# Moving one tile's loads to another queue, cutting the decays in two, and putting additions behind others, in a two-layer trunk of attention and RWKV-7

## The chip, the cores and the metric

The kernel runs on one core of a Trainium2 chip. The metric is the device time of one execution in microseconds (us), and of a few runs the median counts. Engines are named as in the profile: PE is TensorE, DVE is VectorE, ACT is ScalarE, POOL is GpSimd, SP is SyncE.

## The reference

One sequence of 512 tokens with 2048 channels, float32, goes through two residual layers, each `x + W_out(mixer(rms_norm(x)) * silu(gate))`.

```
# layer 0: differential attention, 8 heads of two 128-wide queries and keys, values 256 wide
proj = h @ w_in ; q, k, v, gate = split(proj, 4)
q, k = rope(rms_norm(q)), rope(rms_norm(k))
a = softmax(q0 k0 + causal) - lam * softmax(q1 k1 + causal)
o = rms_norm(a @ v) * (1 - lambda_init) * silu(gate) ; out = o @ w_out
# layer 1: RWKV-7, 32 heads of 64 channels
p = h @ w_in ; p = p + (token_shift(p) - p) * mu ; r, k, v, g, dw, da = split(p)
decay = exp(-exp(-softplus(-(w0 + tanh(dw) @ decay_up)) - 0.5)) ; a = sigmoid(a0 + da @ iclr_up)
kk = normalised(k * k_k) ; k = k * (1 + (a - 1) * k_a)
for each token:  S = S * w_t + (S a_t) b_t + v_t k_t ;  y_t = S r_t     # a_t = -kk, b_t = kk * a
y = group_norm(y) + sum(r * k * r_k) * v ; out = (y * silu(g)) @ w_out
```

## The kernel before

**Matmuls in three parts.** Every operand is split into a high part in the matmul's own format and a low remainder, and a product is three matmuls (high by high, low by high, high by low). For a weight chunk of 512 KB (`wraw`), ACT casts the high part (`wh`, L105) and DVE subtracts to get the low one (`wl`, L106). SP loads the chunks (`load_w`, L78), and POOL's queue makes additions in flight: `add_w` (L86) issues a DMA that adds a second weight chunk onto one that lies in SBUF.

**Layer 0** goes head by head. In `unit_head` the queries, keys, values and gates of one head are formed with seven products of half-size blocks in place of eight, so sums of weight blocks are wanted. The tiles Ta to Td (`g.Ts`) hold a chain of such sums: a product is made with T, then another block is added onto T, and the next product uses it. `all_groups` runs one product over the four chunks i of the contraction, and issues behind chunk i the additions for what comes next: onto T (`then`), and, in the last head alone, onto the four chunks of `b22` too (`also`). POOL issues them in the order in which they are written, since each is put behind the one before (`issue_after`).

While a head's products run on PE, the attention of the head before is woven in by a `Chain`: a generator that counts PE's matmuls and runs its next step when the count is through. `attention` works on four blocks of 128 rows; each step for a block has scores, transposes (L364), the weighted values, and `turn_y`, which writes the turned output as `yTh` (ACT, L399) and `yTl` (DVE, L401) and stores both on ACT's queue (L386) to the HBM tensors `ys`. `yTh` and `yTl` have one buffer each. A further chain (`keys`) turns the new keys with transposes at L296; its delay in matmuls is an argument, 9 and in the last head 20.

**Layer 1** goes over 16 pairs of heads. Pair j's projections fill PE; among them stand the scan of pair j − 1 (`scan_pair`, woven in by a chain: per chunk of 64 tokens the matmuls L1475, L1486 and L1493, and the state's update on DVE, L1497, which the next L1475 needs) and the preparation of pair j + 1.

- `stage1` makes the decays. The list `g.later` holds parts that are run one by one between the chain's steps, each behind the state's update on DVE (0) or ACT's copy (1): `decays` (the scan L1240 and the centring L1242, L1243), `exponentials` (ACT), `queries` (DVE, L1252 to L1254), `scales` (ACT, L1258), `keys` (L1262, L1266 and others).
- `gram` makes the Gram matrix `G` and stores blocks of it to HBM (`ltd`, L1316); `mask_gram` masks it in two halves on POOL (L1325, L1327).
- `t_solve` loads `ltd` back as the tile `LT`, rearranged, with four DMAs on POOL's queue (L1350), and solves a triangular system on DVE in 31 steps of two instructions (L1361, L1363), which end with L1364. The result goes to HBM (`td`, L1365), and `t_combine` loads it as `TT` and transposes it (L1388) for the matmuls L1394 and L1404. The second half of `mask_gram` stands behind the LT loads on POOL.
- `stage_v` makes y (L1418), `finish_y` ends a pair (L1547, L1554).

The Tile framework orders each engine's instructions by the priorities that the code gives (`high_priority` with offsets; the solve has the highest) and by `issue_after`, which puts one instruction behind another.

Of the kernel before, what the change touches and what calls it, by code (L numbers as in the profile page):

```python
# [28 lines left out]
NH = 8  # L29
# [44 lines left out]
def load_w(g, raw, part, k0, ks, queue=None):  # L74

    w, c = part
    with g.tc.issue_after(g.last) if g.last and not queue else ExitStack():
        ld = (queue or g.nc.sync).dma_start(out=raw[:, ks.start : ks.stop], in_=w[c][:, k0 + ks.start : k0 + ks.stop])  # L78
    g.last = ld.ins if g.last and not queue else g.last
    return ld.ins  # L80


def add_w(g, raw, part, k0):

    w, c = part
    return g.nc.gpsimd.dma_start(out=raw[:], in_=w[c][:, k0 : k0 + KG], accum_op=ALU.add).ins  # L86
# [378 lines left out]
KG = 2  # L465
# [66 lines left out]
def unit_head(g, aps, h, t1s, sq, turned):  # L532


    nc = g.nc
# [37 lines left out]
    def all_groups(out, lhs, raw, start=False, end=False, then=None, also=None):  # L573
        added = None
        for i in range(N):
            r = raw(i)
            products(out, lhs(i), r, start and i == 0, end and i == N - 1)
            for x, k0 in [(r, then)] + ([(also[i], (c2, 0))] if also else []) if then else []:
                with g.tc.issue_after(added) if added else ExitStack():
                    added = add_w(g, x, k0[0], k0[1] + i * KG)  # L580

    def s4(out, keep, start=False, end=False):
        def raw(i):
# [212 lines left out]
def layer0(g, aps):  # L796
# [3 lines left out]
    with ExitStack() as cx:  # L800
# [91 lines left out]
        for h in range(NH):  # L892
            if h:
                Chain(g, attention(g, h - 1, *before, 26, keys=rest), 56 if h > 1 else 20)
            t1s = [t1_tile() for _ in range(NT)] if h else t1s
            sq = g.small.tile([P, NT, 2], F32, name="sq", tag="sq")
            qkT = head_qkT(g)

            def keys(n, t1s=t1s, qkT=qkT):
                for t in range(n):  # L900
                    turn_qk(g, t1s, *qkT, t)
                    if t < n - 1:
                        yield 20

            rest = [(g, t1s, *qkT, t) for t in (2, 3)]
            if h:
                values = unit_head(g, aps, h, t1s, sq, lambda: Chain(g, keys(2), 9 if h < NH - 1 else 20))
            else:
                for ts in ([0, 1], [2, 3]):
                    head_qk(g, t1s, sq, ts)  # L910
                Chain(g, keys(2), 120)
                input_sums(g, pairs, False)
                ps = unit_tok(g, g.hH, g.hL, vg_cols(aps, h), 512)
                acc1 = g.work.tile([P, 2, 512], F32, name="acc1", tag="acc1", bufs=1)
                G, vg = gates(g)
# [298 lines left out]
def stage1(g, j, k, up):  # L1214
# [3 lines left out]
    p = Pair()  # L1218
# [20 lines left out]
    def decays():  # L1239
        nc.vector.tensor_tensor_scan(l[:].rearrange("p c t -> p (c t)"), g.rmask[:].rearrange("p c t -> p (c t)"),  # L1240
                                     lw[:], 0.0, ALU.mult, ALU.add)
        nc.vector.tensor_scalar(m[:], l[:, :, C - 1], 0.5, None, ALU.mult)  # L1242
        nc.vector.tensor_sub(l[:], l[:], m[:, :, None].to_broadcast([P, NC_, C]))  # L1243

# [21 lines left out]
        nc.vector.tensor_add(p.gam[:, 0 : NC_ - 1], m[:, 0 : NC_ - 1], m[:, 1:NC_])  # L1266
        nc.scalar.activation(p.gam[:, 0 : NC_ - 1], p.gam[:, 0 : NC_ - 1], AF.Exp)

    g.later += [(0, decays), (1, exponentials), (0, queries), (1, scales), (1, keys)]
    return p  # L1270


# [68 lines left out]
def t_solve(g, j, p):  # L1341
# [5 lines left out]
    Tm = w.tile([P, NQ, HALF], F32, name="Tm", tag="Tm", bufs=1)  # L1347
    tmp = w.tile([P, NQ * HALF], F32, name="tmpl", tag="tmpl", bufs=1)
    for i in range(NG):
        ld = nc.gpsimd.dma_start(out=LT[i * 32 : i * 32 + 32], in_=g.ltd[j % 2].rearrange("b h c s t -> (b h c) s t"))  # L1350
    n2 = LT[:, HALF, :]
    nc.vector.tensor_scalar(n2, n2, 1e-24, None, ALU.max)
    nc.vector.reciprocal(n2, n2)
# [9 lines left out]
        nc.vector.tensor_add(Tm[:, 0:s, i + 1 :], Tm[:, 0:s, i + 1 :], tt)  # L1363
    nc.vector.tensor_mul(Tm[:], Tm[:], n2[:, None, :].to_broadcast([P, NQ, HALF]))  # L1364
    nc.sync.dma_start(out=g.td[j % 2].rearrange("q l t -> l q t"), in_=Tm[:])  # L1365
    return ld.ins


GAP_D, GAP_X, GAP_T = 18, 10, 8
# [189 lines left out]
def layer1(g, aps):  # L1559
    nc, tc = g.nc, g.tc  # L1560
    with ExitStack() as cx:
# [25 lines left out]
        for j in range(D // P):  # L1587
# [15 lines left out]
            def behind(m, j=j, p=p, normed=normed):  # L1603
                if j > 1:
                    pairs[j - 2].chain.finish(g)
                with tc.issue_after(m.ins):
                    gram(g, j, p, j > LAG + 1 and pairs[j - 1].chain)
                p.rfs = split_act(g, p.rf[:], w, "x")
                mask_gram(g, p, 0)
                loaded = t_solve(g, j, p)  # L1610
                with tc.issue_after(loaded):
                    mask_gram(g, p, 1)
                if j > 1 and not normed:
                    group_norm(g, j - 2, pairs[j - 2])

# [6 lines left out]
                first = gate_of(0, "g0")  # L1622
            if j + 1 < D // P:
                begin(j + 1)
            if j > LAG:
                gated(g, j - LAG, pairs[j - LAG], gate_of(j - LAG))
            if j + 1 < D // P:
# [80 lines left out]
def body(ctx, tc, nc, aps):  # L1708
    g = Ctx()
    g.nc, g.tc = nc, tc  # L1710
    g.last, g.first, g.centred = None, [], None
    g.chains, g.later, g.state, g.copied = [], [], None, None
    g.const = ctx.enter_context(tc.tile_pool(name="const", bufs=1))
    g.hp = ctx.enter_context(tc.tile_pool(name="hp", bufs=16))
# [57 lines left out]
```

## Time and profile before

| | |
|---|---|
| median of 3 runs | 2111.32 us (2108.85 to 2113.85) |
| the profiled execution, its own time | 2111.84 us |
| its span | 2110.1 us |
| PE busy | 2076.8 us, 98% |
| DVE, ACT, POOL busy | 1602.6, 1153.6, 370.4 us |
| moved by DMA | 294.60 MB, 140 GB/s over the span |

The profile is of one execution. Span is the time from its first instruction to its last, and its own time stands beside it. A busy engine executes instructions; waiting, branching and issuing DMAs aren't counted. Where a row has a bracket, the engine was idle for so long ahead of it, and the name in it is what came last of that for which it waited.

### The profile page before, as it was taken

To read this page: it belongs to the slowest core of one execution; us is meant where nothing else is said; L and a number is where in the kernel's file an instruction comes from. 1 tells how busy PE (TensorE), PEld (TensorE's weight loads), DVE (VectorE), ACT (ScalarE), POOL (GpSimd) and SP (SyncE) were. 2 spreads that over 40 slices of the span, in tenths; PEclk is the share of its full clock that TensorE was granted. 3 is DMA by queue.
4 is the path that set the end of the run, shared out by engine and by line. 5 is a ranking of instruction groups with operands and counts; after the bars stand their busy time and mean duration, and the time that the engine had idled before them with its cause. 6 is when DMAs were issued, how large, how long until landed. Compare 5 with 4: busy or idle time off the path is not lost.

```text
span 2110.1 us, 34038 instructions
## 1 busy us (share of the span) xinstructions
PE 2076.8 (98%) x11852; PEld 1690.5 (80%) x11852; DVE 1602.6 (76%) x4129; ACT 1153.6 (55%) x2278; POOL 370.4 (18%) x727
## 2 busy tenths in 40 slices
PE   9999999999999999999999999999999999999999
PEld 7888888888887788878777778888877787877887
DVE  6988888889887876576777778877777887767645
ACT  5765656566565544355465555565555556555322
POOL 1021111201112000101122221222222122221001
PEclk9999999999999999999999999999999999999999
DMA  8487877878778946623232332323333232345655
GB/s 268 153 173 190 181 170 187 166 188 177 173 183 176 307 149 179 150 88 96 90 87 89 90 90 84 94 83 92 99 95 86 85 94 86 97 138 180 190 159 121
DMA packets 159484, 294.60 MB, mean 140 GB/s; under 512 B 64352, under 2 KB 81760, under 8 KB 159312
## 3 DMA queue, kind: packets, MB, share of 16 engines
q1 hardware_dynamic: 110848, 184.91, 28.1%
q0 software_dynamic: 23808, 83.54, 21.5%
q10 hardware_dynamic: 24656, 23.97, 3.5%
q8 instruction: 93, 1.52, 0.3%
q14 instruction: 79, 0.65, 0.1%
HBM read 268.71 MB, written 23.66 MB: 139 GB/s over the span
## 4 chain that ended last, share of the span: by engine, by line
PE 74%; DVE 17%; issue 3%; ACT 3%; DMA 2%; ACTq 0%; DVEq 0%; SPq 0%
PE pp L122 33%; PE pp L568 22%; PE pt L122 4%; DVE wl L106 4%; DVE tmpl L1361 3%; DVE Tm L1363 2%; DVE VS L1497 2%; PE gp L1304 1%; ACT wh L105 1%; PE sc L122 1%; PE o L122 1%; PE sm L1475 1%; PE lora L122 1%; PE z L122 1%; PE sm L1486 1%
## 5 line engine op out<-in xcount | busy, mean ns | idle before, releaser
L106 DVE TENSOR_TENSOR wl<-wraw,wh 128x1024 fp32r<-128x1024 f32 (+2 forms) x291 | 357.7, 1229 | 211.0 <-ACT wh L105 202.2
L105 ACT CAST wh<-wraw 128x1024 fp32r<-128x1024 f32 (+2 forms) x291 | 303.6, 1043 | 266.1 <-PE pp L122 135.2
L122 PE MATMUL pp<-hL,wh 128*128 128x512 f32 x1024 | 414.7, 405 | 0.0
L122 PE MATMUL pp<-hH,wh 128*128 128x512 f32 x1024 | 413.8, 404 | 0.0
L122 PE MATMUL pp<-hH,wl 128*128 128x512 f32 x1024 | 413.6, 404 | 0.0
L122 PEld LDWEIGHTS pp<-hH,wh 128*128 128x128 f32 x1024 | 193.6, 189 | 34.3
L122 PEld LDWEIGHTS pp<-hL,wh 128*128 128x128 f32 x1024 | 193.5, 189 | 33.3
L122 PEld LDWEIGHTS pp<-hH,wl 128*128 128x128 f32 x1024 | 193.6, 189 | 32.4
L568 PE MATMUL pp<-wh,hH 128*128 128x512 f32 x448 | 176.8, 395 | 0.0
L568 PE MATMUL pp<-wh,hL 128*128 128x512 f32 x448 | 175.8, 392 | 0.0
L122 PE MATMUL pp<-wh,hH 128*128 128x512 f32 x372 | 145.6, 392 | 1.8 <-ACT hH L1092 1.8
L122 PE MATMUL pp<-wh,hL 128*128 128x512 f32 x372 | 146.4, 394 | 0.2
L122 PE MATMUL pp<-wl,hH 128*128 128x512 f32 x372 | 145.9, 392 | 0.5 <-DVE wl L106 0.5
L1481 POOL COPY SA<-VS 64x64 f32<-64x64 f32 x224 | 69.9, 312 | 425.0 <-DVE VS L1497 386.0
L1361 DVE SCALAR_TENSOR_TENSOR tmpl<-LT,Tm 128x60 f32<-128x60 f32 (+24 forms) x496 | 133.6, 269 | 11.4
L568 PE MATMUL pp<-wl,hH 128*128 128x512 f32 x448 | 140.4, 392 | 0.0
L1363 DVE TENSOR_TENSOR Tm<-Tm,tmpl 128x60 f32<-128x60 f32 (+24 forms) x496 | 104.4, 211 | 11.3
L1478 ACT COPY rhs<-sm 64x64 f32<-64x64 f32 x256 | 52.8, 206 | 89.3 <-PE sm L1475 85.9
L568 PEld LDWEIGHTS pp<-wl,hH 128*128 128x128 f32 x448 | 84.4, 188 | 17.3
L568 PEld LDWEIGHTS pp<-wh,hH 128*128 128x128 f32 x448 | 84.2, 188 | 17.3 <-issue 0.3
L568 PEld LDWEIGHTS pp<-wh,hL 128*128 128x128 f32 x448 | 84.2, 188 | 16.3
L1488 ACT COPY VS<-sm 64x64 f32<-64x64 f32 x256 | 52.7, 206 | 71.9 <-PE sm L1486 67.3
(397 smaller groups left out, 4417.6 us busy)
## 6 DMA issues: line engine op xcount, KB each, us to landing
wraw<-in_rw_w_in_dram SPq DMA_DIRECT2D x128, 512.0 KB
wraw<-in_da_w_in_dram SPq DMA_DIRECT2D x75, 512.0 KB
wraw<-in_da_w_in_dram POOLq DMA_DIRECT2D x28, 512.0 KB, 6.6
wraw<-in_da_w_out_dram SPq DMA_DIRECT2D x26, 512.0 KB
wraw<-in_rw_w_out_dram SPq DMA_DIRECT2D x26, 512.0 KB
Ta<-in_da_w_in_dram POOLq DMA_DIRECT2D x21, 512.0 KB, 5.5
Tb<-in_da_w_in_dram POOLq DMA_DIRECT2D x21, 512.0 KB, 5.5
Tc<-in_da_w_in_dram POOLq DMA_DIRECT2D x21, 512.0 KB, 5.5
```

The source lines that it names most:

```text
L105: a = nc.scalar.copy(hi[:, ks], raw[:, ks])
L106: d = nc.vector.tensor_sub(lo[:, ks], raw[:, ks], hi[:, ks].bitcast(F32))
L122: m = nc.tensor.matmul(out, a, b, start=s, stop=e, skip_group_check=skip)
L568: m = nc.tensor.matmul(out[t][:], x, wt[lo][:, k, :], start=first, stop=end and lo == 1 and k == KG - 1, skip_group_check=True)
L1304: m = nc.tensor.matmul(gp[h][:, i * P : (i + 1) * P], BK[r_, c0 + i, :, :], p.AR[r_, c0 + i, :, :], start=True, stop=True)
L1361: nc.vector.scalar_tensor_tensor(tt, LT[:, i : i + 1, i + 1 :].to_broadcast([P, s, n]), n2[:, i : i + 1], Tm[:, 0:s, i : i + 1].to_broadca ...
L1363: nc.vector.tensor_add(Tm[:, 0:s, i + 1 :], Tm[:, 0:s, i + 1 :], tt)
L1475: nc.tensor.matmul(sm[:, 0:P], both(p.G[:, c, 0]), both(VS[:, c]), start=True, stop=True)
L1478: nc.scalar.copy(rhs[r_, :], sm[r_, h * C : h * C + C])
L1481: nc.gpsimd.tensor_copy(p.SA[r_, c - 1, :], VS[r_, c, h, :])
L1488: g.copied = nc.scalar.copy(VS[r_, c, h, :], sm[r_, P : P + C])
L1497: g.state = nc.vector.scalar_tensor_tensor(VS[r_, c + 1, h, :], s_, p.gam[r_, c : c + 1], Sg[r_, :], ALU.mult, ALU.add)
```

## The change

There are three parts.

1. *Layer 0, last head.* The additions onto b22 stood one behind each addition onto T. Now there is none behind chunks 0 and 1, b22[0] stands behind chunk 2, and b22[1], b22[2] and b22[3] behind chunk 3. The delay of the chain that turns the keys is 24 matmuls in the last head, 20 before.
2. *LT.* The four loads of LT go on SP's queue. `p.loaded` keeps the last of them, and `g.held` is set to it, so that weights which `load_w` issues later on SP stand behind it. The second half of `mask_gram` no longer stands behind the loads.
3. *Decays.* `decays` is cut in two: the scan, and `centres` (L1242, L1243). The list `later` runs decays, scales, centres, exponentials, queries, keys, where it ran decays, exponentials, queries, scales, keys.

```diff
@@ load_w
-    with g.tc.issue_after(g.last) if g.last and not queue else ExitStack():
+    behind = g.held if queue is None and not g.last else g.last if not queue else None
+    with g.tc.issue_after(behind) if behind else ExitStack():
@@ all_groups
-            for x, k0 in [(r, then)] + ([(also[i], (c2, 0))] if also else []) if then else []:
+            adds = [(r, then, i)] if then else []
+            if also:
+                adds += [(also[n], (c2, 0), n) for n in ((), (), (0,), (1, 2, 3))[i]]
+            for x, k0, n in adds:
                 with g.tc.issue_after(added) if added else ExitStack():
-                    added = add_w(g, x, k0[0], k0[1] + i * KG)
+                    added = add_w(g, x, k0[0], k0[1] + n * KG)
@@ layer0
-                values = unit_head(g, aps, h, t1s, sq, lambda: Chain(g, keys(2), 9 if h < NH - 1 else 20))
+                values = unit_head(g, aps, h, t1s, sq, lambda: Chain(g, keys(2), 9 if h < NH - 1 else 24))
@@ stage1
     def decays():
         nc.vector.tensor_tensor_scan(l[:].rearrange("p c t -> p (c t)"), g.rmask[:].rearrange("p c t -> p (c t)"),
                                      lw[:], 0.0, ALU.mult, ALU.add)
+
+    def centres():
         nc.vector.tensor_scalar(m[:], l[:, :, C - 1], 0.5, None, ALU.mult)
         nc.vector.tensor_sub(l[:], l[:], m[:, :, None].to_broadcast([P, NC_, C]))
...
-    g.later += [(0, decays), (1, exponentials), (0, queries), (1, scales), (1, keys)]
+    g.later += [(0, decays), (1, scales), (0, centres), (1, exponentials), (0, queries), (1, keys)]
@@ t_solve
-        ld = nc.gpsimd.dma_start(out=LT[i * 32 : i * 32 + 32], in_=g.ltd[j % 2].rearrange("b h c s t -> (b h c) s t"))
+        p.loaded = nc.sync.dma_start(out=LT[i * 32 : i * 32 + 32], in_=g.ltd[j % 2].rearrange("b h c s t -> (b h c) s t")).ins
...
-    return ld.ins
@@ layer1
-                loaded = t_solve(g, j, p)
-                with tc.issue_after(loaded):
-                    mask_gram(g, p, 1)
+                t_solve(g, j, p)
+                mask_gram(g, p, 1)
...
             if j + 1 < D // P:
                 begin(j + 1)
+            g.held = p.loaded
```

More of the change, by code (lines that the diff above doesn't have):

```diff
@@ L1710, in body @@
     g.nc, g.tc = nc, tc
-    g.last, g.first, g.centred = None, [], None
+    g.last, g.held, g.first, g.centred = None, None, [], None
     g.chains, g.later, g.state, g.copied = [], [], None, None
```

## The prediction

> **What bounds the kernel now.** The page comes first, its span and its first section, for which engine is the limit.
>
> ```profile
> span 2110.1 us, 34038 instructions
> PE 2076.8 (98%) x11852; PEld 1690.5 (80%) x11852; DVE 1602.6 (76%) x4129; ACT 1153.6 (55%) x2278; POOL 370.4 (18%) x727
> ```
>
> TensorE (PE) works 2076.8 of 2110.1 us, so all its idle time is 33.3 us. The change gives PE the same matmuls. It can win or lose only in those 33 us, or where the clock is down. The next view is PE's list of waits: the line that waited, what released it, then the total, the number and the longest, in us.
>
> ```profile
> PE sm L1475 <- DVE VS L1497: 9.7, 28, 0.8
> PE pt L364 <- DVE rs_i L65: 5.8, 1, 5.8
> ...
> PE px L1394 <- DVE y L1418: 1.2, 1, 1.2
> ...
> PE px L1394 <- DVE T L1388: 0.8, 1, 0.8
> PE gp L1304 <- DVE AR L1279: 0.7, 1, 0.7
> PE pt L1554 <- DVE yc L1547: 0.7, 2, 0.4
> ```
>
> The adds to b22 bear on the single 5.8. The loads of T's solution (tile LT) and the decays bear on the second layer, where 28 short waits make 9.7. For the clock I read the table of stretches; behind the window and its length stand the busy times of PE, PEld, DVE, ACT and POOL, then the granted clock, the DMA share and GB/s.
>
> ```profile
> 687.80:692.20 4.40, 4.40 (x13) 3.62 (x14) 4.09 (x16) 1.53 (x2) 0.00 (x0) 0.50 1.08 216
> ...
> 1027.00:1030.00 3.00, 3.00 (x8) 2.32 (x8) 2.78 (x4) 2.01 (x5) 1.21 (x2) 0.50 0.24 63
> ```
>
> After two of the waits PE runs at half clock. The 4.4 us from 687.80 cost half of themselves, 2.2, so the stall at L364 is worth 5.8 + 2.2 = 8.0 us. The profiled execution took 2111.84 us, 0.5 above the median of 2111.32. The sum is made against 2111.84, and 0.5 comes off at the end.
>
> **Adds to b22 in the last head.** The rows are of the timelines of POOL, ACT, DVE and PE (start, duration, engine, line; in brackets the idle time before and its releaser), and the last is of the list of who waited for the tensor ys.
>
> ```profile
> 672.24 0.86 POOL L86 DMA_DIRECT2D Tb<-in_da_w_in_dram  x1 [1.38 <-DVE yTl L401]
> 672.77 1.21 POOL L86 DMA_DIRECT2D wraw<-in_da_w_in_dram  x1
> 678.29 0.84 POOL L86 DMA_DIRECT2D Tc<-in_da_w_in_dram  x1 [4.30 <-ACT sc L350]
> ...
> 671.28 0.37 ACTq L386 DMA_DIRECT2D ys<-yTh  x1
> 672.55 0.37 ACTq L386 DMA_DIRECT2D ys<-yTl  x1
> 681.93 0.62 ACT L399 ACTIVATE yTh<-yt,subw 128x128 fp32r<-128x128 f32 x2 [2.36 <-DMA ys<-yTh]
> ...
> 687.08 0.35 DVE L401 SCALAR_TENSOR_TENSOR yTl<-yt,subw,yTh 128x128 fp32r<-128x128 f32 x1 [7.07 <-DMA ys<-yTl]
> ...
> 696.45 0.35 DVE L401 SCALAR_TENSOR_TENSOR yTl<-yt,subw,yTh 128x128 fp32r<-128x128 f32 x1
> ...
> 687.80 1.11 PE L364 MATMUL pt<-ident,a 128*128 128x128 f32 x4 [5.81 <-DVE rs_i L65]
> ...
>   DVE yTl L401: 7.4, 2
> ```
>
> The 5.8 is not a wait for weights. The attention of the head before stores yTh and yTl of each block of 128 rows, and each tile has one buffer. Block 0's stores were issued at 671.28 and 672.55. They released the next writers at 681.93 and 687.08, that is 10.6 and 14.5 us later, while POOL's additions of 512 KB each were in flight. L401 of block 1 waited 7.07 us, and PE behind it 5.81. Of all stores of yTl only two held L401, 7.4 us in all, so this one is nearly the whole of it: stores without such company are out in time.
>
> In the new order POOL issues Ta, Tb, Tc, b22[0], Td, b22[1], b22[2], b22[3]; so far an addition to b22 follows each of Ta to Td. Two of them thus leave block 0's stores. Tc can hardly go before 678.29, since its row waits for work of that moment, and so block 0's stores share with Ta and Tb alone. L401 of block 1 is then on time, and the 8.0 us are won at this place. But the four additions have not gone. From 678.3 on six stand in a row, and block 1's stores, issued at about 680 and 681 without the stall, meet them all. Its yTl is out at 681 + 14.5 = 695.5 if it fares as block 0's did, at 681 + 10.6 = 691.6 by the row of yTh. L401 of block 2 stands at 696.45 now and would be ready 8.0 sooner, at 688.5, so DVE is held 3.1 to 7.0 us. Of 7.07 PE felt 5.81, which leaves 1.3 of cover, and PE loses 1.8 to 5.7. The clock adds 0 to 2.2. I take 5.5 and 1.5, near the row of yTl, since the company is denser than it was: −8.0 + 7.0 = **−1.0 us**, between −8.0 (no hold) and +0.5 (the same hold with less cover). The keys' delay of 24 matmuls in place of 20 puts four matmuls ahead of the first transposes of keys; PE has the same work, so nothing.
>
> **First pairs: SyncE's queue, and the solve ahead of a cast.** From the list of tile LT, the timelines of DVE and PE, and the page's groups:
>
> ```profile
> L1350 POOL DMA_DIRECT2D LT<-ltd x64: 489/499/556, 975.6 to 1876.8; - x64
> ...
>   DMA ltd<-G: 23.4, 11
> ...
> 983.64 0.25 DVE L1361 SCALAR_TENSOR_TENSOR tmpl<-LT,Tm 128x30 f32<-128x30 f32 x1
> 987.20 1.23 DVE L106 TENSOR_TENSOR wl<-wraw,wh 128x1024 fp32r<-128x1024 f32 x1 [3.31 <-ACT wh L105]
> 988.35 0.18 DVE L1363 TENSOR_TENSOR Tm<-Tm,tmpl 128x30 f32<-128x30 f32 x1
> ...
> 989.89 0.22 DVE L1363 TENSOR_TENSOR Tm<-Tm,tmpl 128x54 f32<-128x54 f32 x1
> ...
> 1025.42 1.09 PE L1394 MATMUL px<-T,G 32*32 32x32 f32 x32 [1.15 <-DVE y L1418]
> 1026.44 0.55 PE L122 MATMUL pp<-hH,wh 128*128 128x512 f32 x1
> 1026.79 0.63 PE L122 MATMUL pp<-hL,wh 128*128 128x512 f32 x1
> ...
> 1029.78 0.58 PE L122 MATMUL pp<-hH,wl 128*128 128x512 f32 x1
> ...
> L105 ACT CAST wh<-wraw 128x1024 fp32r<-128x1024 f32 (+2 forms) x291 | 303.6, 1043 | 266.1 <-PE pp L122 135.2
> ```
>
> In pair 0 the solve stands still on DVE for 3.31 us: its order puts a weight's L106 between two halves of a step, and L106 waits for the cast. In the changed order of DVE the steps from 988.35 to the one ending at 990.11 stand ahead of that L106. They fill 1.76 of the 3.31 us, and the solve of pair 0, its stores and loads, and the two transposes and y behind them end 1.8 us sooner. PE's wait of 1.15 for y and the 0.7 for AR, both behind the same solve on DVE, are shorter than that and go. The half clock from 1026.79 to 1030.2, 3.4 us long and costing 1.7, follows the first wait and should go with it. That is −1.15 − 0.7 − 1.7, about **−3.5 us**, between −3.5 and 0 (nothing comes sooner).
>
> SyncE takes 64 issues of 0.5 us, four in a pair, and the wait for G's landing in HBM, 23.4 us in 11 pairs, or 2.1 each. Weights queued behind LT leave up to 2.1 + 2.0 = 4.1 us later once in a pair. The cover is that the cast L105 waits mostly for PE to free wh (135.2 us of 266.1), not for raw weights. I take nothing; with the cover gone it costs at most 4.1 in a pair. POOL's second mask, so far behind the LT loads, comes sooner and nobody waits for it.
>
> **Later pairs: decays in two parts.** Rows of DVE's and PE's timelines in pair 7:
>
> ```profile
> 1407.40 0.17 DVE L1242 TENSOR_SCALAR m<-l 128x8 f32<-128x8 f32 x1
> ...
> 1407.66 0.68 DVE L1243 TENSOR_TENSOR l<-l,m 128x512 f32<-128x512 f32 x1
> ...
> 1408.46 0.16 DVE L1266 TENSOR_TENSOR gam<-m 128x7 f32<-128x7 f32 x1
> ...
> 1409.15 0.23 DVE L1363 TENSOR_TENSOR Tm<-Tm,tmpl 128x66 f32<-128x66 f32 x1
> 1409.42 0.28 DVE L1361 SCALAR_TENSOR_TENSOR tmpl<-LT,Tm 128x60 f32<-128x60 f32 x1
> ...
> 1416.01 1.22 DVE L1262 TENSOR_TENSOR BK<-BK,l 128x1024 f32<-128x1024 f32 x1
> ...
> 1410.48 0.46 PE L1475 MATMUL sm<-VS,G 128*128 128x128 f32 x2 [0.49 <-DVE VS L1497]
> ...
> 1421.73 0.46 PE L1475 MATMUL sm<-VS,G 128*128 128x128 f32 x2 [0.18 <-DVE VS L1497]
> ```
>
> DVE has no idle time here, so what stands ahead of an L1497 delays it. Ahead of the first, 0.17 + 0.68 + 0.16 = 1.01 us of centring leave and three halves of solve steps come in, about 0.23 + 0.28 + 0.28 = 0.79: the wait of 0.49 becomes about 0.25. The moved part then stands ahead of the last L1497, with L1262 nearer to it. The exponentials run one state later on ACT, and what needs them on DVE follows. I let the wait of 0.18 grow by 0.2. Per pair that is −0.24 + 0.20 = −0.04, times 14 pairs **−0.5 us**, between −9.4 (both waits gone, 14 × 0.67) and +10 (the rival below).
>
> At the end the waits for T (0.8) and yc (0.7) see scan matmuls one to three places earlier in PE's order; I take **−0.5** of their 1.5, between −1.5 and +1.
>
> **Sum.** 2111.84 − 1.0 − 3.5 − 0.5 − 0.5 = 2106.3; less the 0.5, 2105.8, so **2106 us**. By itself this case is good for 2102 to 2109.5. A measurement of this kernel can tell about 0.2%, 4.2 us, from no change: faster is below 2107.1, slower above 2115.5.
>
> **The rivals.**
> - *The stall goes altogether.* Block 1's stores slip through while Tc's data are still to come, and L401 of block 2 is on time. For it: no store elsewhere holds anyone longer than 0.4 us. Against it: the rows of 10.6 and 14.5 us with fewer additions beside them. 7.0 less than my case: 2099.
> - *Slower: L1262 reaches the last L1497.* The centring comes one state later, so the 1.22 us of L1262 move toward the last L1497 of each pair, where PE waits 0.18 already and has no cover. If L1497 stands behind it by more than the 0.24 won at the first wait, the pair loses; behind it by 0.8 more, 14 × 0.8 = 11 us are lost: 2106 + 11 = 2117. Against it: between the last two pairs of L1497 PE has the length of two gaps.
> - *The change misses its places.* The solve's fill of 1.8 us is eaten by what stands behind it, and the stall returns whole: 2111.84 − 0.5 − 0.5 − 0.5, 2110.
> - *The half clock of pair 0 stays.* Only the waits, 1.8, go, and not the 1.7 behind them: 2107.5. The trace has a stop of 1.15 us and then clock 0.50 within 1.4 us, so a short stop is followed by half clock here. The Trainium skill ("TensorE: Matmul & The Clock Gate", "What's actually happening") has the clock fall only after at least one idle window of about 3.4 us; by that rule the stop at 1024 could not be the cause and its removal would leave the 1.7 where they are. The trace speaks against the rule, as PE had no longer stop there.
>
> **Chances.** My case 0.52, of which 0.36 lies under 2107.1; the stall gone 0.17; slower 0.12; the places missed 0.14; the half clock staying 0.05, about 0.02 of it below the line. Faster: 0.36 + 0.17 + 0.02 = 0.55. Slower 0.12. Within 0.2%: the rest, 0.33. The range reaches from 2098, under the case of the stall gone, to 2113, above the case of missed places; it leaves out the slower case and a little below, under 2 in 10.
>
> **What would show it.** PE's wait at L364 gone from its list, and a wait of 2 to 6 us near 690, released by way of L401 with "DMA ys<-yTl" in its bracket. DVE's idle time ahead of the first wl in pair 0 near 1.5 in place of 3.31, no wait at L1394 for y, and clock 1.00 from 1027 to 1030. The 9.7 of L1475 between 8 and 11. I am wrong if PE's list has no wait above 1 us near 690, if L1475's sum passes 14, or if L105 waits for weights in the second layer.

## The result and the profile after

The changed kernel takes 2129.49 us in the median of 4 runs (2125.14 to 2130.61); the kernel before, with the runs made beside it, 2112.59 (2108.85 to 2116.19). The ratio is 1.0076, 95% interval 1.0053 to 1.01: slower by 0.76%, where 2106 and "faster" stood. The profiled execution took 2129.91 us, 18.1 more than the one of before.

The first lines of the page after, and PE's list of waits after. The functions have moved by one to six lines: L105 and L106 are now L106 and L107, L122 is L123, L364 is L365, L401 is L402, L568 is L569, L1262 is L1268, L1361 and L1363 are L1367 and L1369, L1388 is L1393, L1394 is L1399, L1475 is L1480, L1497 is L1502, L1547 and L1554 are L1552 and L1559.

```profile
span 2128.2 us, 33996 instructions
...
PE 2081.6 (98%) x11852; PEld 1697.1 (80%) x11852; DVE 1614.6 (76%) x4129; ACT 1152.4 (54%) x2278; POOL 336.4 (16%) x663
```

```profile
PE sm L1480 <- DVE VS L1502: 15.0, 35, 1.0
PE pp L569 <- ACT wh L106: 6.6, 1, 6.6
PE pt L1559 <- DVE yc L1552: 5.3, 2, 5.0
PE pp L123 <- ACT wh L106: 3.6, 1, 3.6
...
PE px L1399 <- DVE y L1423: 2.1, 1, 2.1
```

The wait of 5.8 at L364 is gone, and so is the 0.7 for AR. In their place stand 6.6 at L569, 5.0 at L1559 and 3.6 at L123. The state's waits grew from 9.7 to 15.0 and the wait for y from 1.2 to 2.1. PE's own busy time rose by 4.8 us for the same 11852 matmuls: worked out from the PE rows, by 3.2 in the first 40 us and by 2.4 in the last pair, and elsewhere it changed little. The table of stretches after (window, length, busy PE, PEld, DVE, ACT, POOL, then the granted clock, DMA share, GB/s) shows the clock at these places:

```profile
20.00:26.00 6.00, 5.00 (x11) 3.51 (x12) 3.98 (x5) 3.84 (x6) 0.00 (x0) 0.55 1.04 400
702.40:706.00 3.60, 3.60 (x9) 2.65 (x10) 3.60 (x9) 1.40 (x2) 0.00 (x0) 0.50 1.05 384
1030.70:1034.70 4.00, 4.00 (x12) 2.91 (x10) 2.01 (x4) 2.55 (x5) 0.00 (x0) 0.57 0.88 263
1892.00:1896.00 4.00, 3.13 (x11) 2.35 (x9) 3.83 (x10) 0.57 (x3) 0.00 (x0) 0.50 0.44 149
1934.00:1938.00 4.00, 4.00 (x12) 3.32 (x13) 4.00 (x7) 2.39 (x5) 0.00 (x0) 0.50 0.47 128
```

Half clock follows four of the waits (6.6, 2.1, 3.6 and 5.0), and one row is at the very start, before anything that the change touches.

To place the difference I took the start of each PE matmul in one trace less the start of the same matmul (the k-th of its kind) in the trace of before: the lag. Its growth from stage to stage, in us, worked out from the PE rows of one profiled execution of each kernel (medians over the 10 us that begin at 650, 750, 1000, 1040, 1850 and 1950, in the time of before):

| kernel | start of layer 0, to 650 | last head's adds, 650 to 750 | pair 0, 1000 to 1040 | later pairs, 1040 to 1850 | last pair, 1850 to 1950 |
|---|---|---|---|---|---|
| predicted | 0 | −1.0 | −3.5 | −0.5 | −0.5 |
| after | +3.4 | +0.5 | +0.5 | +4.7 | +9.1 |
| p_adds | +2.8 | +0.3 | +0.2 | +0.2 | +5.3 |
| p_decays | +2.3 | −1.6 | −1.4 | +8.5 | +1.7 |
| p_lt | +2.2 | −1.2 | +0.6 | +2.3 | +8.6 |
| after_no_hold_last | +2.3 | +1.9 | +0.3 | +5.1 | −2.7 |
| no_b22_adds | −1.0 | −8.0 | 0.0 | +0.2 | 0.0 |
| lt_mask_behind | +1.8 | +0.1 | +0.6 | +2.4 | +8.2 |
| lt_ends | −0.9 | +0.4 | −1.7 | +0.2 | −3.3 |
| keys_earlier | +1.1 | −1.7 | −1.8 | +3.3 | −0.4 |
| lt_mask_wait | +2.0 | −0.8 | 0.0 | +14.7 | +10.2 |
| keys_last | +2.0 | −1.3 | 0.0 | −5.5 | +0.1 |
| decays_keys_last | +1.4 | −1.5 | −1.3 | +5.0 | −0.1 |
| decays_keys_ends | +0.9 | −1.4 | +0.8 | +2.2 | −3.0 |
| after_mended | +0.9 | +1.5 | −1.3 | −7.4 | −3.4 |
| keys_last_ends | −0.6 | 0.0 | +0.3 | −5.3 | −3.3 |

The first column is of parts that are the same in all these kernels. It runs from −1.0 to +3.4, so it is a difference between executions, and 3.4 of the 18.1 us are no effect of the change. The change itself cost 14.7 in this execution: 9.1 in the last pair, 4.7 in the later pairs, 0.5 each in pair 0 and at the adds. By the medians of the runs it cost 16.9.

**The last head after.** Timelines of POOL, ACT, DVE and PE:

```profile
681.69 0.86 POOL L87 DMA_DIRECT2D Tc<-in_da_w_in_dram  x1 [5.07 <-ACT sc L351]
...
684.23 2.94 POOL L87 DMA_DIRECT2D wraw<-in_da_w_in_dram  x3
...
684.20 0.37 ACTq L387 DMA_DIRECT2D ys<-yTl  x1
...
683.50 0.35 DVE L402 SCALAR_TENSOR_TENSOR yTl<-yt,subw,yTh 128x128 fp32r<-128x128 f32 x1
700.03 0.35 DVE L402 SCALAR_TENSOR_TENSOR yTl<-yt,subw,yTh 128x128 fp32r<-128x128 f32 x1 [8.18 <-DMA ys<-yTl]
...
702.30 0.79 PE L569 MATMUL pp<-wh,hH 128*128 128x512 f32 x1 [6.58 <-ACT wh L106]
```

Block 1 is on time (683.50). Its store of yTl, issued at 684.20, among six additions, lets the next writer go at 700.03, 15.8 us later, and DVE is held for 8.18. PE loses 6.58, and then works at clock 0.50.

**Pair 0 after.** Timelines of POOL, DVE and PE:

```profile
1015.98 1.36 POOL L1331 TENSOR_SCALAR_AFFINE_SELECT G<-G 64x512 f32<-64x512 f32 x2 [34.86 <-ACT G L1317]
1017.31 2.37 POOL L1333 TENSOR_SCALAR_AFFINE_SELECT G<-G 64x1024 f32<-64x1024 f32 x2
...
1016.71 0.67 DVE L1369 TENSOR_TENSOR Tm<-Tm,tmpl 128x28 f32<-128x28 f32 x1
...
1018.53 1.17 DVE L1369 TENSOR_TENSOR Tm<-Tm,tmpl 128x24 f32<-128x24 f32 x1
1019.73 0.24 DVE L1367 SCALAR_TENSOR_TENSOR tmpl<-LT,Tm 128x16 f32<-128x16 f32 x1
...
1029.65 1.09 PE L1399 MATMUL px<-T,G 32*32 32x32 f32 x32 [2.06 <-DVE y L1423]
```

Both halves of the mask of pair 1's G now run in one stretch, beside the end of pair 0's solve, from 1015.98 to 1019.68, and just there four steps of the solve take 0.67 to 1.17 us; the next one, behind the masks, takes 0.24. Before, the first half alone ran beside the solve (1013.00 to 1014.78), and two steps took 0.65 and 1.08.

**Pair 7 after**, timelines of DVE and PE:

```profile
1425.40 1.22 DVE L1268 TENSOR_TENSOR BK<-BK,l 128x1024 f32<-128x1024 f32 x1
1426.54 0.59 DVE L1502 SCALAR_TENSOR_TENSOR VS<-sm,gam,Sg 64x64 f32<-64x64 f32 x2
...
1415.32 0.46 PE L1480 MATMUL sm<-VS,G 128*128 128x128 f32 x2 [0.29 <-DVE VS L1502]
1427.28 0.46 PE L1480 MATMUL sm<-VS,G 128*128 128x128 f32 x2 [0.74 <-DVE VS L1502]
```

The first wait fell from 0.49 to 0.29. The last rose from 0.18 to 0.74, and the instruction right ahead of its L1502 is L1268, the old L1262.

**Last pair after**, timelines of SyncE's queue, DVE and PE, and behind them weights' issues of before:

```profile
1882.00 1.70 SPq L1356 DMA_DIRECT2D LT<-ltd  x4
1883.75 1.37 SPq L79 DMA_DIRECT2D wraw<-in_rw_w_in_dram  x3
...
1930.70 0.44 DVE L1393 STREAM_TRANSPOSE T<-TT 64x256 f32<-64x256 f32 x1 [6.72 <-DMA TT<-td]
...
1891.26 0.80 PE L123 MATMUL pp<-hH,wh 128*128 128x512 f32 x1 [3.60 <-ACT wh L106]
```

```profile
1863.24 0.33 SPq L78 DMA_DIRECT2D wraw<-in_rw_w_in_dram  x1
...
1873.25 0.35 SPq L78 DMA_DIRECT2D wraw<-in_rw_w_in_dram  x1
```

Before, weights left SyncE at 1863.24 and 1873.25, ahead of the loads of LT (from 1875.32, on POOL). The trace of after lags by some 9 us here, and in it no weight leaves between 1851.00 and LT's loads: three go together from 1883.75, and PE waits 3.60. Part of that wait comes by way of ACT, whose timeline has, after:

```profile
1889.55 0.72 ACT L1424 ACTIVATE y<-y,prm_hgb 128x512 f32<-128x512 f32 x1 [1.62 <-DVE y L1423]
1890.18 1.98 ACT L106 CAST wh<-wraw 128x1024 fp32r<-128x1024 f32 x2
```

By the trace's DMA packets the first of the three weights was through at about 1887.5, as PE stopped (1887.66). The cast that PE waits for still came only at 1890.18, since y stands ahead of it on ACT. Later in the pair T's transpose (L1393) waits 6.72 for its data on DVE, ahead of what is left of yc, and that is the 5.0 at L1559.

### The profile page after: what moved, and what is told of

The parts are those of the page before. It is cut to its first block, busy times and chain, and to the rows that moved or that the text cites. A ratio compares the mean times of both kernels' runs of the same rounds, so it can differ in the third digit from the quotient of the medians.

```text
span 2128.2 us, 33996 instructions
## 1 busy us (share of the span) xinstructions
PE 2081.6 (98%) x11852; PEld 1697.1 (80%) x11852; DVE 1614.6 (76%) x4129; ACT 1152.4 (54%) x2278; POOL 336.4 (16%) x663
## 4 chain that ended last, share of the span: by engine, by line
PE 76%; DVE 16%; DMA 3%; issue 3%; ACT 2%; SPq 0%; ACTq 0%; DVEq 0%; POOLq 0%; POOL 0%
PE pp L123 35%; PE pp L569 22%; PE pt L123 5%; DVE tmpl L1367 3%; DVE wl L107 3%; DVE Tm L1369 3%; DVE VS L1502 2%; PE sm L1480 1%; PE sc L123 1%; PE gp L1310 1%; PE o L123 1%; ACT wh L106 1%; PE lora L123 1%; PE z L123 1%; PE sm L1491 1%
## 5 line engine op out<-in xcount | busy, mean ns | idle before, releaser
L107 DVE TENSOR_TENSOR wl<-wraw,wh 128x1024 fp32r<-128x1024 f32 (+2 forms) x291 | 357.4, 1228 | 210.3 <-ACT wh L106 204.5
L106 ACT CAST wh<-wraw 128x1024 fp32r<-128x1024 f32 (+2 forms) x291 | 303.5, 1043 | 268.7 <-PE pp L123 128.3
L123 PE MATMUL pp<-hH,wh 128*128 128x512 f32 x1024 | 414.6, 405 | 3.6 <-ACT wh L106 3.6
L123 PE MATMUL pp<-hL,wh 128*128 128x512 f32 x1024 | 416.0, 406 | 0.0
L123 PE MATMUL pp<-hH,wl 128*128 128x512 f32 x1024 | 415.1, 405 | 0.9 <-DVE wl L107 0.9
L123 PEld LDWEIGHTS pp<-hH,wh 128*128 128x128 f32 x1024 | 194.6, 190 | 38.9 <-ACT wh L106 4.0
L123 PEld LDWEIGHTS pp<-hH,wl 128*128 128x128 f32 x1024 | 194.4, 190 | 34.2 <-DVE wl L107 1.6
L123 PEld LDWEIGHTS pp<-hL,wh 128*128 128x128 f32 x1024 | 194.4, 190 | 34.1
L569 PE MATMUL pp<-wh,hH 128*128 128x512 f32 x448 | 178.0, 397 | 6.6 <-ACT wh L106 6.6
L569 PE MATMUL pp<-wh,hL 128*128 128x512 f32 x448 | 176.6, 394 | 0.0
L123 PE MATMUL pp<-wh,hH 128*128 128x512 f32 x372 | 147.2, 396 | 2.4 <-ACT hH L1096 2.4
L123 PE MATMUL pp<-wl,hH 128*128 128x512 f32 x372 | 147.1, 395 | 0.5 <-DVE wl L107 0.5
L123 PE MATMUL pp<-wh,hL 128*128 128x512 f32 x372 | 147.4, 396 | 0.1
L1367 DVE SCALAR_TENSOR_TENSOR tmpl<-LT,Tm 128x60 f32<-128x60 f32 (+24 forms) x496 | 135.5, 273 | 13.6
L569 PE MATMUL pp<-wl,hH 128*128 128x512 f32 x448 | 140.8, 393 | 0.0
L1486 POOL COPY SA<-VS 64x64 f32<-64x64 f32 x224 | 61.8, 276 | 473.3 <-DVE VS L1502 402.1
L1369 DVE TENSOR_TENSOR Tm<-Tm,tmpl 128x60 f32<-128x60 f32 (+24 forms) x496 | 105.2, 212 | 12.3
L569 PEld LDWEIGHTS pp<-wh,hH 128*128 128x128 f32 x448 | 84.7, 189 | 24.2 <-ACT wh L106 7.0
L569 PEld LDWEIGHTS pp<-wl,hH 128*128 128x128 f32 x448 | 84.7, 189 | 17.6 <-DVE wl L107 0.4
L569 PEld LDWEIGHTS pp<-wh,hL 128*128 128x128 f32 x448 | 84.8, 189 | 16.5
```

Source lines behind the costliest of these rows:

```text
L106: a = nc.scalar.copy(hi[:, ks], raw[:, ks])
L107: d = nc.vector.tensor_sub(lo[:, ks], raw[:, ks], hi[:, ks].bitcast(F32))
L123: m = nc.tensor.matmul(out, a, b, start=s, stop=e, skip_group_check=skip)
L569: m = nc.tensor.matmul(out[t][:], x, wt[lo][:, k, :], start=first, stop=end and lo == 1 and k == KG - 1, skip_group_check=True)
L1367: nc.vector.scalar_tensor_tensor(tt, LT[:, i : i + 1, i + 1 :].to_broadcast([P, s, n]), n2[:, i : i + 1], Tm[:, 0:s, i : i + 1].to_broadca ...
L1486: nc.gpsimd.tensor_copy(p.SA[r_, c - 1, :], VS[r_, c, h, :])
```

## The experiments

Ratios are to the kernel before in the same set, with the 95% interval. First the parts of the change one by one.

**p_adds**: the new order of the additions and the delay of 24 alone.

```diff
+            adds = [(r, then, i)] if then else []
+            if also:
+                adds += [(also[n], (c2, 0), n) for n in ((), (), (0,), (1, 2, 3))[i]]
...
```

> Only the new order of additions and the delay of 24 in the kernel before. Theory (the hold of the store tile moves one block on): PE's wait of 5.8 us at L364 goes, a wait of 5 to 8 us comes some 10 us later, released by way of the store of yTl; total 0 within 2 us of the kernel before. Rival (the additions gained what they could and the loss is all elsewhere): no wait above 1 us near 690, 6 to 8 us faster.

2115.0 us, ratio 0.9999 (0.9987 to 1.001). PE's list of waits:

```profile
PE pp L568 <- ACT wh L105: 6.5, 1, 6.5
```

Of the writers of yTl one was held, for 8.1 us. The wait has moved on by a block and kept its size, and the time stays. (Its last pair, where nothing was changed, took 5.3 us more in the profiled execution, the slowest of its ten runs, with clock 0.50 from 1927.7 to 1938.0. So far can that stage go by itself.)

**p_decays**: the decays cut in two and the new list alone.

```diff
+    def centres():
...
-    g.later += [(0, decays), (1, exponentials), (0, queries), (1, scales), (1, keys)]
+    g.later += [(0, decays), (1, scales), (0, centres), (1, exponentials), (0, queries), (1, keys)]
```

> Only the decays in two parts, in the kernel before. Theory (the last state of each pair waits behind L1262 on DVE): the two waits per pair at L1475 go from 0.49 and 0.18 to about 0.3 and 0.75, sum of that line about 14 to 15 us in place of 9.7, 4 to 6 us slower, last pair as before. Rival (the later pairs lose by SyncE's queue): waits at L1475 as before, no difference.

2123.78 us, ratio 1.0044 (1.0031 to 1.0057): slower by itself, by more than the 4 to 6 us expected. PE's list, and PE's timeline in pair 7:

```profile
PE sm L1477 <- DVE VS L1499: 18.3, 35, 1.2
```

```profile
1411.83 0.46 PE L1477 MATMUL sm<-VS,G 128*128 128x128 f32 x2 [0.56 <-DVE VS L1499]
1417.52 0.46 PE L1477 MATMUL sm<-VS,G 128*128 128x128 f32 x2 [0.15 <-DVE VS L1499]
1423.79 0.46 PE L1477 MATMUL sm<-VS,G 128*128 128x128 f32 x2 [0.74 <-DVE VS L1499]
```

The three waits make 1.45 where 0.67 stood: 0.78 more in this pair. Without the LT part, the first wait does not even fall.

**p_lt**: LT on SyncE's queue, the weights held behind it, and the second mask free, alone.

```diff
+    behind = g.held if queue is None and not g.last else g.last if not queue else None
...
-        ld = nc.gpsimd.dma_start(out=LT[...], ...)
+        p.loaded = nc.sync.dma_start(out=LT[...], ...).ins
...
+            g.held = p.loaded
...
```

> Only LT on SyncE with the weights behind it and the second mask free, in the kernel before. Theory (weights of the last pair stand behind its LT): PE waits 3 to 5 us for wh near 1885 and 4 to 5 us for yc near 1925, 8 to 10 us slower in the last pair; in pair 0 the second mask on POOL slows two steps of the solve and the wait for y is 1.2 to 2.1 us. Rival (the last pair is late through the decays): last pair as before, within 2 us in all.

2123.63 us, ratio 1.0036 (1.0024 to 1.0048). PE's list:

```profile
PE pt L1554 <- DVE yc L1547: 4.9, 2, 4.6
...
PE pp L123 <- ACT wh L106: 3.6, 1, 3.6
...
PE px L1394 <- DVE y L1418: 2.1, 1, 2.1
```

Three of the new waits of the changed kernel are here, with nearly the same lengths: they belong to this part. The later pairs lose 2.3 us too, with the decays whole. Timelines of DVE and PE in pair 7:

```profile
1423.05 0.41 DVE L1365 TENSOR_TENSOR Tm<-Tm,LT 128x256 f32<-128x256 f32 x1
...
1423.93 0.46 PE L1475 MATMUL sm<-VS,G 128*128 128x128 f32 x2 [0.72 <-DVE VS L1497]
```

The first wait is 0.19 (0.49 before) and the last 0.72 (0.18). L1262 is not near that last update, but the solve's last instruction, L1365, stands between the two instructions of the update (1422.86 and 1423.49).

**after_no_hold_last**: the changed kernel, but in the last pair the weights are not put behind LT.

```diff
-            g.held = p.loaded
+            if j + 1 < D // P:
+                g.held = p.loaded
```

> The changed kernel, but in the last pair the weights do not stand behind LT on SyncE. Theory: the 3.6 us for wh near 1888 go; the 5.0 for yc near 1929 goes too if it came from the bunched weights and TT behind them; 5 to 9 us faster than the changed kernel, 6 to 12 slower than the one before. Rival (LT itself on SyncE is late there): both waits stay within 1 us.

2117.16 us, ratio 1.0007 (0.9996 to 1.0018): 12.3 us less than the changed kernel, by one line, where 5 to 9 were expected; it can no longer be told from the kernel before. SyncE's timeline in the last pair:

```profile
1872.10 0.33 SPq L79 DMA_DIRECT2D wraw<-in_rw_w_in_dram  x1
...
1883.56 1.70 SPq L1356 DMA_DIRECT2D LT<-ltd  x4
```

Weights leave ahead of LT again, and the waits of 3.6 and 5.0 are both gone. The hold had also changed the order on ACT: here the casts of the first two of those weights (1880.44 and 1889.07) stand ahead of y (1891.47). With LT on SyncE but no hold in this pair, the last pair is 2.7 us faster than before.

**no_b22_adds**: the kernel before without the four additions onto b22 (their sum is left out of the result).

```diff
-            for x, k0 in [(r, then)] + ([(also[i], (c2, 0))] if also else []) if then else []:
+            for x, k0 in [(r, then)] + [] if then else []:
```

> The kernel before without the four additions onto b22 (that part of the last head's weights is left out of the sum). Theory (the additions keep the DMA engines so busy that the stores of yTh and yTl are late): no wait at L364 or for wh between 675 and 710, no half clock there, 5 to 8 us faster than the kernel before. Rival (the additions onto T alone are enough to hold the stores): a wait above 2 us stays there.

2103.5 us, ratio 0.9958 (0.994 to 0.9975), and no wait of PE at L364 or L568. Who waited for ys:

```profile
  ACT yTh L399: 0.8, 1
```

Without the company the stores are out in time. What the additions cost before is 8.0 us in the lag, the value that the prediction gave the stall, and 8.8 by the medians.

**lt_mask_behind**: p_lt, with the second mask put behind the LT load again.

```diff
-                mask_gram(g, p, 1)
+                with tc.issue_after(p.loaded):
+                    mask_gram(g, p, 1)
```

> LT on SyncE with the weights behind it, but the second half of the mask put behind the LT loads again. Theory (the second mask on POOL slows two solve steps of pair 0): in pair 0 no step of the solve above 0.7 us beside one mask, the wait for y at L1394 under 0.5 us in place of 2.1, 3 us less there than with LT alone; the last pair as slow as with LT alone. Rival (the mask doesn't matter, SyncE's loads of T are late): the wait for y stays near 2.

2123.13 us, ratio 1.006 (1.0045 to 1.0075). POOL's timeline:

```profile
1013.77 1.36 POOL L1326 TENSOR_SCALAR_AFFINE_SELECT G<-G 64x512 f32<-64x512 f32 x2 [34.66 <-ACT G L1312]
```

The two halves of the mask still ran together, well ahead of that load on SyncE: put behind an instruction of another engine's queue in this way, the mask did not wait for it here. So this run does not test the mask; lt_mask_wait does.

**lt_ends**: the kernel before, with LT on SyncE in the first and the last pair only, and no hold.

```diff
-        ld = nc.gpsimd.dma_start(out=LT[...], ...)
+        ld = (nc.sync if j in (0, D // P - 1) else nc.gpsimd).dma_start(out=LT[...], ...)
```

> LT on SyncE in the first and last pair alone, no weights held behind it, the mask behind it as before. Theory: later pairs as in the kernel before (0.49 and 0.18 at L1475), pair 0 gains up to 3 us where the solve stands ahead of the cast, last pair 0 to 3 us faster; 0 to 5 us faster in all. Rival (SyncE's queue costs wherever LT is on it): the last pair loses 2 us or more.

2110.77 us, ratio 0.9993 (0.9984 to 1.0003): not to be told from no change in the median, though in the profiled execution pair 0 gains 1.7 and the last pair 3.3. PE's timeline in pair 0, and the table of stretches behind the wait:

```profile
1024.70 1.09 PE L1394 MATMUL px<-T,G 32*32 32x32 f32 x32 [1.22 <-DVE y L1418]
```

```profile
1025.70:1029.70 4.00, 4.00 (x48) 3.20 (x45) 2.74 (x4) 2.96 (x6) 1.65 (x2) 1.00 0.33 94
```

The wait for y is as long as before (1.22 beside 1.15), and the clock behind it stays at 1.00. The half clock of pair 0 thus doesn't hang on the wait's length alone.

**keys_earlier**: the kernel before, with scales and exponentials run as one part, so that the keys come sooner.

```diff
-    g.later += [(0, decays), (1, exponentials), (0, queries), (1, scales), (1, keys)]
+    g.later += [(0, decays), (1, scaled), (0, queries), (1, keys)]
```

> The kernel before with scales and exponentials in one part, so that keys (with L1262) comes one state earlier, where the change made it one later. Theory (the place of the 1.22 us of L1262 against the last state decides the wait there): the wait of 0.18 ahead of the last L1475 goes, that of 0.49 stays, L1475's sum 6 to 8 us in place of 9.7, 2 us faster. Rival (it is the centring, not L1262, or DVE's load alone): 0.18 stays or grows.

2116.47 us, ratio 1.0019 (1.0005 to 1.0032): a little slower, where 2 us faster was expected. PE's timeline in pair 7:

```profile
1415.63 0.46 PE L1479 MATMUL sm<-VS,G 128*128 128x128 f32 x2 [0.51 <-DVE VS L1501]
```

The last wait (0.18) is gone, and a new one of 0.51 stands at the middle chunk: the keys' long instructions sit ahead of another L1501.

**lt_mask_wait**: p_lt, with a copy of one column of LT on POOL (into an unused column) ahead of the second mask, so that the mask truly waits for LT.

```diff
+                seen = nc.gpsimd.tensor_copy(p.gam[:, NC_ - 1 : NC_], p.LT[:, 0, 0:1]).ins
+                with tc.issue_after(seen):
                     mask_gram(g, p, 1)
```

> LT on SyncE as in the kernel with LT alone, and on POOL one added copy of one column of LT ahead of the second mask, so that POOL really waits for LT's landing there. Theory (the second mask of pair 1 slows the end of pair 0's solve): two slow steps of about 0.65 and 1.1 us in place of four, the solve of pair 0 about 33.2 us in place of 34.6, the wait for y at L1394 near 1 us or below in place of 2.1. Rival: solve and wait as with LT alone.

2135.94 us, ratio 1.0098 (1.0083 to 1.0112). Timelines of DVE and PE in pair 0:

```profile
1013.70 0.62 DVE L1365 TENSOR_TENSOR Tm<-Tm,tmpl 128x28 f32<-128x28 f32 x1
1014.35 1.08 DVE L1363 SCALAR_TENSOR_TENSOR tmpl<-LT,Tm 128x24 f32<-128x24 f32 x1
...
1026.59 1.09 PE L1395 MATMUL px<-T,G 32*32 32x32 f32 x32 [1.64 <-DVE y L1419]
```

With one half of the mask at 1013.63 to 1015.41 there are two slow steps in place of four. From its first step to the end of its last, the solve of pair 0 takes 32.75 us; it took 33.60 before, 34.55 after and 34.58 in p_lt. Of the 1.8 us between p_lt and this run 0.4 were there before the masks ran, so the second half beside the solve costs 1.4, which is shown. But the wait for y falls only from 2.1 to 1.64, and not below 1 as expected: from the issue of the first load of TT to the transpose of T 4.83 us passed (1019.44 to 1024.27), and 4.07 before. The later pairs lose 14.7 us: there the waiting mask comes to lie beside the solve, and 23 of its steps take over 0.5 us, where before none did. In all 16 profiled executions no step of a solve took over 0.5 us but beside a mask.

**keys_last**: the kernel before, with the keys run behind the state's update in place of the copy.

```diff
-    g.later += [(0, decays), (1, exponentials), (0, queries), (1, scales), (1, keys)]
+    g.later += [(0, decays), (1, exponentials), (0, queries), (1, scales), (0, keys)]
```

> The kernel before with keys (L1262) put behind the last state's update on DVE, all else as it was. Theory (L1497 waits in line behind long DVE work): the wait of 0.49 stays, that of 0.18 goes; L1475's sum about 7 us, 2 to 3 us faster. Rival (something behind keys, the square of k or the transposes of BK, is late then): a new wait after the last state, no gain.

2107.24 us, ratio 0.9969 (0.9954 to 0.9984): faster. PE's list:

```profile
PE sm L1475 <- DVE VS L1497: 4.3, 18, 0.5
```

Not by the mechanism that I had written: the update comes ahead of the next copy, so the keys moved half a step earlier. L1262 kept its place; a following operand of 0.69 us went from 1422.9 to 1415.88, one of 0.73 us that stood ahead of the last L1497 fell behind it, and L1266 (0.16 us) left its place ahead of the first L1497. In pair 7 the waits of 0.49 and 0.18 became 0.19 and none.

**decays_keys_last** (p_decays with `(0, keys)` at the end of its list) and **decays_keys_ends** (the same, with LT on SyncE in the first and last pair, as in lt_ends).

> Decays in two parts as in the change, but keys (L1262) behind the last state's update in place of ahead of it; nothing else changed. Theory (the 1.22 us of L1262 ahead of the last state is what the later pairs lose): the 0.74 at the last L1475 goes and about 0.3 at the first stays, L1475's sum 4 to 7 us in place of 18; 10 to 14 us faster than the decays alone, 2 to 5 faster than the kernel before. Rival (the centring itself or ACT's new order costs): the last wait stays above 0.5.

> The same with LT on SyncE in the first and last pair, no weights held behind it. Theory: the gains add, 4 to 9 us faster than the kernel before: later pairs 3 to 5, pair 0 about 1.7, last pair 0 to 3. Rival (they share one gain): no more than the better of the two alone.

2120.62 us, ratio 1.003 (1.0016 to 1.0043), and 2112.55, ratio 0.9991 (0.9981 to 1.0002). PE's timeline in pair 7 of the first:

```profile
1422.33 0.46 PE L1477 MATMUL sm<-VS,G 128*128 128x128 f32 x2 [0.28 <-DVE VS L1499]
```

Taking L1262 away from the last L1497 brings that wait from 0.74 to 0.28; the first stays at 0.56 (1410.83). The three waits of the pair still make 1.02, where 0.67 stood before and 0.19 in keys_last. The split of the decays thus costs more than the neighbour of the last update, and both runs missed "faster".

**after_mended** (after_no_hold_last with the decays whole, and before's list with `(0, keys)`) and **keys_last_ends** (keys_last with lt_ends).

```diff
-    g.later += [(0, decays), (1, scales), (0, centres), (1, exponentials), (0, queries), (1, keys)]
+    g.later += [(0, decays), (1, exponentials), (0, queries), (1, scales), (0, keys)]
...
+            if j + 1 < D // P:
+                g.held = p.loaded
```

> The changed kernel with two of its causes taken out: in the last pair the weights do not stand behind LT, and the decays are in one part with keys behind the last state's update. Theory (these two make the loss; the additions and the second mask move little): the waits of 3.6 and 5.0 in the last pair and the 0.74 at the last L1475 are gone, 18 to 23 us faster than the changed kernel and up to 4 us faster than the one before. Rival (LT on SyncE with weights behind it costs in every pair by itself): still 3 us or more slower than the kernel before.

> Keys behind the last state's update as in keys_last, and LT on SyncE in the first and last pair alone. Theory (the gains lie in different stretches and add): 1 to 5 us faster than keys_last, 7 to 11 faster than the kernel before. Rival (the moved keys take the last pair's gain): as keys_last.

2102.97 us, ratio 0.996 (0.9946 to 0.9974), and 2104.01, ratio 0.9963 (0.9948 to 0.9978). Both beat both kernels: after_mended is 9.3 us under before and 26.5 under the changed kernel, more than the 4 and the 18 to 23 expected. Some 6 of that are the moved keys, which gain by themselves (keys_last). PE's list of the first:

```profile
PE pp L569 <- ACT wh L106: 6.8, 1, 6.8
```

LT on SyncE with the hold in every pair but the last costs nothing here (−7.4 in the later pairs, beside −5.3 with LT on POOL), though it cost 2.3 with the keys in their old place (p_lt). So the rival that it costs in each pair whatever the order falls. The adds' stall is still there, 6.8. keys_last_ends came as expected, 3.2 under keys_last.

## Why the prediction was wrong

**What bounds the kernel** stood: PE's busy time is fixed but for the clock, and all of the change lies in its waits.

**Adds to b22: −1.0 predicted, +0.5 measured**, on the upper bound. Each step happened: the wait at L364 gone, L402 of block 1 on time, block 1's stores issued 3.2 and 3.5 us after the 681 and 680 of the prediction (the start's lag is 3.4), L402 of block 2 ready at 700.03 − 8.18 = 691.85, which less 3.4 is the 688.5 forecast. Mis-sized was the store: 15.8 us where 14.5 was taken, so DVE was held 8.18 (3.1 to 7.0 given) and PE 6.58 (1.8 to 5.7). There is a second fault, a smaller one: the 8.0 was read from one execution. The other kernels with the old order and the additions stand at −1.7 to +0.4 against it in this stage, −0.9 in the mean of ten; the four with the new order at +0.3 to +1.9, mean +1.05. In this stage the new order is thus about 2 us worse; the medians of p_adds are too coarse to tell that.

**First pairs: −3.5 predicted, +0.5 measured.** The 0.7 for AR went, the step that held. The failed step is "POOL's second mask … comes sooner and nobody waits for it": it came beside the solve. Counted from the solve's first step, the steps ran 1.5 us ahead of before's at first, near the 1.8 worked out; about 1 us was lost again midway, and two further slow steps cost 1.4, so that the solve took 34.55 us in place of 33.60. The Trainium skill ("SBUF — State Buffer", "Who interferes with whom") states that a DVE instruction with two SBUF inputs contends with a GpSimd instruction that reads SBUF, and that contention for the ports they share is an exclusive lock. The trace agrees: steps of 0.18 to 0.25 us took 0.67 to 1.17 just while the masks ran, and lt_mask_wait halved their number. The rows have the operands of both, and I did not put them side by side. The other failed step is the clock, "should go with it". The half clock stayed, as in the rival to which I gave 0.05, and here the wait stayed too. PE has this wait in all 16 profiled executions. Eleven have half clock behind stops of 1.14 to 2.21 us, and five have none behind stops of 0.77, 1.22, 1.22, 1.33 and 1.86. The trace shows that a short stop can be followed by half clock, as the prediction read it, but not that every one is: taking 1.7 us as sure was wrong. The length alone does not decide it, but the traces show what goes with it. In each of them all changes of the granted clock lie on one grid of 3.41 us, which lies elsewhere in each execution. Where 1.14 us or more of this stop fell into one cell of the grid (the eleven), the next cell had clock 0.50; where it was 1.07 or less (the five), it had 1.00. The stop of 1.15 before, 1024.26 to 1025.42, lies whole in the cell from 1023.33 to 1026.75. The longer one of after_mended is cut by the grid at 1027.05 into 0.83 and 1.04, and its clock stayed at 1.00:

```profile
1028.08 1.09 PE L1397 MATMUL px<-T,G 32*32 32x32 f32 x32 [1.86 <-DVE y L1421]
```

For other stops the same count is no sharp rule: p_decays has 1.22 us idle in the cell from 697.7, and no half clock behind it. Why the wait for y stayed above 1.1 in all variants but keys_earlier is open.

**Later pairs: −0.5 predicted, +4.7 measured.** The first wait fell to 0.29 (0.25 forecast). The last rose by 0.56, not 0.20: the failed step is "with L1262 nearer to it", for L1268 stands right ahead of the last L1502. Pair 7 loses 0.56 − 0.20 = 0.36, and 14 × 0.36 is 5.0, close to the 4.7. L1480's sum is 15.0, past the 14 that the prediction named as a sign of being wrong. It is the rival to which I gave 0.12, at less than half of its price. "The length of two gaps" between the last updates, my reason against it, was no protection, since its operands come when the list runs them and DVE has no idle time. p_decays alone loses 8.5 and p_lt alone 2.3, so the parts do not add: with LT's part the first wait is lower (0.29 after, 0.19 in p_lt, 0.56 in p_decays). That p_lt loses in these pairs at all is a second failed step, for LT's move was put at nothing there. Its last wait is 0.72 with L1262 in its old place, as the solve's last instruction came into the update, so L1262 is not the only neighbour that can do this.

**End and SyncE's queue: −0.5 predicted, +9.1 measured; the largest error.** The failed step is "I take nothing; with the cover gone it costs at most 4.1 in a pair". That counted only what the queue itself takes, the issues and the wait for G's landing. But the change puts weights behind LT in order, and so weights that would have left 12 to 26 us sooner (at 1857.88, 1865.04 and 1872.10 in after_no_hold_last, which lags about as much) wait until the solve's data exist, and leave from 1883.75. In the earlier pairs PE did not stop for that; in the last pair it gave 3.6, in part through the order on ACT, and the 5.0 at L1559 came with it. Where nothing holds weights in the last pair, LT on SyncE wins 2.7 to 3.4 there (five kernels); with the hold it loses 8.2 to 10.2 (four kernels). That the hold is the cause is shown by after_no_hold_last. It makes T's data late some 40 us further on: from the store of T to its first transpose 13.55 us pass after (1917.15 to 1930.70), 6.64 before and 7.11 in after_no_hold_last. Both halves are longer, the time until TT's loads are issued (5.3 us, 2.6 before) and the time until they are in (8.2, 4.0 before). Which transfers were in their way is open, and so is why the last pair alone stood still.

**The range** missed by 16 us because no rival spoke of held weights, though the diff says it in a line, and the rivals' prices were not added up: two of them, L1262 at the last update and the half clock of pair 0, came about in one kernel.

## What to carry to other kernels

An order that puts a stream of loads behind one load delays them to the moment at which that load's data exist; price it by how far ahead of that moment they leave now, in every pair by itself, since here only the last one stopped for it, and not by the queue's occupancy. When a step loses its wait, look at what it will then run beside on the other engines, operand by operand, before counting it as free. A stall read from one execution should be compared with the same stall in other executions before it becomes a term of a sum.

## What the runs showed of the hardware

- Stores of yTl and additions of 512 KB in flight: a store was out 14.5 us after its issue in the old order and 15.8 us in the new, so additions moved behind later ones moved the stall without shrinking it; without the additions onto b22 no writer of yTl waited at all.
- Granted clock 0.50 starts 1.0 to 2.3 us after the end of a stop of PE of only 1.1 to 2.2 us in pair 0, in eleven executions of 16. Changes of the clock lie on a grid of 3.41 us, and at this stop 1.14 us idle within one cell were enough and 1.07 were not. The Trainium skill ("TensorE: Matmul & The Clock Gate", "What's actually happening") gives a free-running window of about 3.4 us, and has the clock fall after at least one idle window. The grid agrees with the window; that a whole window must be idle does not, since no stop at this place reached 3.4 us.
- The same first 30 us of the program took up to 3.8 us more in one execution than in another, with clock 0.55 and 1.00 from 20 to 26 us.
